# Decoder step kernel: the first weight load on ScalarE's queue, and the second weight chunk loaded in one piece

## The chip, the cores and the metric

The kernel runs on one core of a Trainium2 chip. The time is the device time of one execution in microseconds (us), the median of three runs; lower is better. Engines are named as the profile names them: PE (TensorE, with PEld for its weight loads), DVE (VectorE), ACT (ScalarE), POOL (GpSimd) and SP (SyncE, which here issues DMA transfers). A row such as "SPq" is the time in which a queue issues a DMA, not the transfer itself.

## The reference, cut to what matters

One inference step of a two-layer decoder over 256 prompt tokens and 64 sample tokens (8 groups of 8), width 1024. Layer 0 mixes tokens with a chunked spatial gate, layer 1 with an mLSTM memory; each is followed by a gated MLP with a short causal convolution. The change touches the very start of layer 0 alone: the normalised input times the `v` half of `a_w_in`.

```
def chunk_spatial_gating(x, w_in, ln_g, ln_b, w_s, b_s, w_out):
    bsz, s, _ = x.shape
    h = jax.nn.gelu(x @ w_in)
    u, v = jnp.split(h, 2, axis=-1)
    ...
def trunk(x, ...):
    for i in range(DEPTH):
        h = rmsnorm(x, norm_mix_g[i])
        if i % N_MIXERS == 0:
            y, v = chunk_spatial_gating(h, ...)
        ...
        x = x + y
        h = rmsnorm(x, norm_ffn_g[i])
        y, fb = conv_ffn(h, ...)
        x = x + y
```

## The kernel before

All 320 tokens (T) are worked on together. The activations lie transposed, 128 features to a block, as eight rows of 320 tokens; "x0" to "x7" below are these eight rows, each the transfer of 160 KB that `x_in` issues (line 382), except x0, which is issued in `run` (line 1274) and carries 16 columns of gains as well (336 columns, 168 KB).

Float32 products are made from two parts of each operand, a high one and a low one. So a chunk of weights comes in as `raw`, ACT casts it to the high part `wh` (line 176, or 171 for the first two chunks), and DVE subtracts to get the low part `wl` (lines 177 and 173). For x, `norm_block` makes the high part `xh` on ACT (line 262) and the low part `xl` on DVE (line 263), and POOL copies the 64 sample columns of both into `xs_a` (lines 386 and 387), behind `xl` for the second copy. PE multiplies only these parts (line 80, the helper `mm`).

The list of weights is made in `weights`; `prefetch(n, m)` sees to it that n chunks have been issued for loading and m have been split. "w0" is chunk 0 (block 0 of `a_wv`, the first four of eight feature blocks, 256 KB), "w1" is chunk 1 (block 4, same feature blocks), "w2" is chunk 2 (block 0, the other four feature blocks), "w3" chunk 3, and so on. `raw` has four buffers, so the load of w4 waits until w0 has been split, w5 until w1 has, and so on. `hold` pins instructions of the start to the order in which the program is written.

Only w0 and w1 are handled in halves: each half is two feature blocks, 128 x 256 numbers, 128 KB. Their loads are four transfers on SP, behind x0. In splitting, DVE makes the first high part of w0 itself (line 168) before `x_parts(0)`, and the other three halves' high parts are ACT casts (line 171); the four low parts are DVE's (line 173). `natural`, which is called for groups of 512 output columns (group 0: w0, later w2 and others; group 1: w1), takes the two halves of such a chunk one after the other, with all tokens for the first half before the second half.

Ahead of that work, `run` issues x0, then `prefetch(2, 0)`, then on ACT a one-column activation `warm` (line 1278) with the table load that it needs, and on PE seven products of constants. SP's order at the start is x0, the four halves, x1, w2, x2, w3, x3, w4, and so on, all on one queue.

Of the kernel before, what the change touches and what calls it, by code (L numbers as in the profile page):

```python
# [58 lines left out]
class Net:  # L59
# [84 lines left out]
    def prefetch(self, n, m):  # L144

        nc = self.nc
        while len(self.loaded) < min(n, len(self.wq)):
            w, b, k0, kn = self.wq[len(self.loaded)]
            raw = self.wraw.tile([P, 8, P], F32, tag="raw", name="raw")
            if isinstance(b, tuple):  # L150
                n = kn // len(b)
                for j, m_ in enumerate(b):
                    self.last_load = nc.sync.dma_start(raw[:, j * n:j * n + n, :], w[m_, :, k0:k0 + n, :])
            else:
                for j, z in ((0, 2), (2, 4)) if len(self.loaded) < 2 else ((0, kn),):
                    self.last_load = self.hold(nc.sync.dma_start(raw[:, j:z, :], w[b, :, k0 + j:k0 + z, :]))  # L156
            self.loaded.append(raw)
        while len(self.halved) < min(m, len(self.wq)):
            i = len(self.halved)
            raw, kn = self.loaded[i], self.wq[i][3]  # L160
            self.loaded[i] = None
            wh = self.wsp.tile([P, 8, P], F32R, tag="wh", name="wh")
            wl = self.wsp.tile([P, 8, P], F32R, tag="wl", name="wl")
            if i < 2:

                a, z = slice(0, 2), slice(2, 4)
                if not i:
                    self.hold(nc.vector.tensor_copy(wh[:, a, :], raw[:, a, :]))
                    self.x_parts(0)
                for c in (a, z)[not i:]:  # L170
                    self.last_split = self.hold(nc.scalar.copy(wh[:, c, :], raw[:, c, :]))
                for c in (a, z):
                    self.last_low = self.hold(nc.vector.tensor_tensor(wl[:, c, :], raw[:, c, :], wh[:, c, :].bitcast(F32), op=SUB))
                self.halved.append((wh, wl))
                continue
            self.last_split = self.hold(nc.scalar.copy(wh[:, :kn, :], raw[:, :kn, :]))  # L176
            self.last_low = nc.vector.tensor_tensor(wl[:, :kn, :], raw[:, :kn, :], wh[:, :kn, :].bitcast(F32), op=SUB)  # L177
            self.hold(self.last_low)
            self.halved.append((wh, wl))
# [1227 lines left out]
```

## Time and profile before

| | us |
|---|---|
| median of three runs | 882.41 (882.1 to 882.59) |
| profiled execution, its own time | 883.35 |
| its span, first to last instruction | 881.6 |
| PE busy in the span | 874.3 (99%) |
| DVE, ACT, POOL busy | 670.7, 512.5, 118.8 |
| granted TensorE clock | 0.998 |

A profile row gives the start, the length, the engine, the line, the operation, what it writes and reads, and how many were merged into the row; in brackets at its end stands how long the engine had been idle before it and what released it. Adjacent instructions of one kind are merged, and matmul ends are modelled, so the pace of PE is best read from one start to the next.

### The profile page before, as it was taken

The numbers are of one execution on the slowest core, as the hardware profiler recorded it, in microseconds if no ns is written. First come the engines' busy times: TensorE is split into PE (matmuls) and PEld (weight loads), VectorE is DVE, ScalarE is ACT, GpSimd is POOL, SyncE is SP. The second block draws the span as 40 slices with busy tenths as digits, with TensorE's granted clock in tenths as the row PEclk, the third lists the DMA queues.
The fourth block names the chain that finished last, engine by engine and source line by source line (L and its number), as shares of the span: only waits on it lengthen the run. The fifth ranks groups of instructions, "written<-read, shape, count | busy, mean of one in ns | idle before, by whom it ended". The sixth has DMA issues, their size and how long they took to land.

```text
span 881.6 us, 17001 instructions
## 1 busy us (share of the span) xinstructions
PE 874.3 (99%) x6423; PEld 857.1 (97%) x6423; DVE 670.7 (76%) x1291; ACT 512.5 (58%) x930; POOL 118.8 (13%) x288
## 2 busy tenths in 40 slices
PE   9999999999999999999999999999999999999997
PEld 7889999999999999999999999999999999999997
DVE  5866986678878865558999998878988788786443
ACT  6658554455555544347777775656766555554442
POOL 3300000020000000002433222303001000000000
PEclk9999999999999999999999999999999999999999
DMA  7755645544454455554746876665664544555551
GB/s 248 245 177 166 184 149 169 177 152 161 167 168 156 156 163 168 160 163 149 244 154 225 248 218 223 197 210 169 192 224 145 167 160 153 168 161 164 156 151 60
DMA packets 55238, 155.76 MB, mean 177 GB/s; under 512 B 7492, under 2 KB 13260, under 8 KB 55156
## 3 DMA queue, kind: packets, MB, share of 16 engines
q1 hardware_dynamic: 55156, 154.67, 55.0%
q8 instruction: 51, 0.84, 0.4%
q14 instruction: 31, 0.25, 0.1%
HBM read 142.66 MB, written 11.99 MB: 175 GB/s over the span
## 4 chain that ended last, share of the span: by engine, by line
PE 98%; DMA 1%; SPq 0%; DVE 0%; issue 0%; ACT 0%; POOL 0%; ACTq 0%
PE pm L80 84%; PE pv_a L80 6%; PE num L80 2%; PE pmix L80 1%; PE pcs L80 1%; PE psc L80 1%; DMA raw<-in_a_wv 1%; PE pCp L80 1%; PE phn L83 1%; PE pv L83 1%; PE pc L80 0%; PE pk L83 0%; SPq L156 0%; DVE y_p L686 0%; PE pg L80 0%; PE pb L80 0%
## 5 line engine op out<-in xcount | busy, mean ns | idle before, releaser
L177 DVE TENSOR_TENSOR wl<-raw,wh 128x1024 fp32r<-128x1024 f32 (+4 forms) x254 | 299.3, 1180 | 115.2 <-ACT wh L176 112.5
L176 ACT CAST wh<-raw 128x1024 fp32r<-128x1024 f32 (+4 forms) x254 | 255.5, 1006 | 215.7 <-PE pm L80 145.9
L80 PE MATMUL pm<-xh,wh 128*128 128x320 f32 x1216 | 356.4, 301 | 0.0
L80 PE MATMUL pm<-xl,wh 128*128 128x320 f32 x1216 | 354.5, 299 | 0.0
L80 PE MATMUL pm<-xh,wl 128*128 128x320 f32 x1216 | 308.8, 299 | 0.0
L80 PEld LDWEIGHTS pm<-xh,wh 128*128 128x128 f32 x1216 | 229.9, 189 | 0.1
L80 PEld LDWEIGHTS pm<-xl,wh 128*128 128x128 f32 x1216 | 229.9, 189 | 0.1
L80 PEld LDWEIGHTS pm<-xh,wl 128*128 128x128 f32 x1216 | 212.0, 189 | 0.0
L80 PE MATMUL pm<-yh_f,wh 128*128 128x320 f32 x352 | 105.2, 299 | 0.0
L80 PE MATMUL pm<-yl_f,wh 128*128 128x320 f32 x352 | 105.2, 299 | 0.0
L80 PE MATMUL pm<-yh_f,wl 128*128 128x320 f32 x352 | 105.2, 299 | 0.0
L80 PEld LDWEIGHTS pm<-yh_f,wh 128*128 128x128 f32 x352 | 66.5, 189 | 0.0
L80 PEld LDWEIGHTS pm<-yl_f,wh 128*128 128x128 f32 x352 | 66.5, 189 | 0.0
L80 PEld LDWEIGHTS pm<-yh_f,wl 128*128 128x128 f32 x352 | 66.5, 189 | 0.0
L592 DVE SCALAR_TENSOR_TENSOR fcv<-fpad,vecs,fcv 128x336 f32<-128x336 f32 x88 | 49.6, 565 | 2.1 <-ACT fcv L590 0.7
L594 ACT ACTIVATE fgl<-fcv 128x256 f32<-128x256 f32 x44 | 18.3, 416 | 37.5 <-DVE fcv L592 37.5
L80 PE MATMUL pm<-yh_a,wh 128*128 128x320 f32 x128 | 38.4, 300 | 0.0
L80 PE MATMUL pm<-yl_a,wh 128*128 128x320 f32 x128 | 38.3, 299 | 0.0
L80 PE MATMUL pm<-yh_a,wl 128*128 128x320 f32 x128 | 38.3, 299 | 0.0
L346 DVE TENSOR_TENSOR xT<-pm,xT 128x320 f32<-128x320 f32 x39 | 19.0, 487 | 24.4 <-PE pm L80 24.4
L80 PE MATMUL pm<-yhb,wh 128*128 128x320 f32 x128 | 35.9, 304 | 0.0
L80 PE MATMUL pm<-ylb,wh 128*128 128x320 f32 x128 | 35.5, 300 | 0.0
(272 smaller groups left out, 1262.9 us busy)
## 6 DMA issues: line engine op xcount, KB each, us to landing
raw<-in_f_up SPq DMA_DIRECT2D x88, 512.0 KB, 3.3
raw<-in_b_win SPq DMA_DIRECT2D x48, 512.0 KB, 4.2
raw<-in_f_dn SPq DMA_DIRECT2D x32, 448.0 KB, 3.3
C<-in_C SPq DMA_DIRECT2D x32, 258.0 KB, 5.3
out_Cs<-C SPq DMA_DIRECT2D x32, 258.0 KB, 4.6
raw<-in_a_win SPq DMA_DIRECT2D x16, 512.0 KB, 3.3
raw<-in_a_wo SPq DMA_DIRECT2D x16, 512.0 KB, 3.9
raw<-in_f_dn SPq DMA_DIRECT2D x16, 512.0 KB, 3.6
```

Of the source, the lines that this page charges most:

```text
L80: self.pin(self.nc.tensor.matmul(out, lhsT, rhs, start=start, stop=stop, skip_group_check=skip))
L83: self.pin(self.nc.tensor.transpose(out, in_, ident))
L176: self.last_split = self.hold(nc.scalar.copy(wh[:, :kn, :], raw[:, :kn, :]))
L177: self.last_low = nc.vector.tensor_tensor(wl[:, :kn, :], raw[:, :kn, :], wh[:, :kn, :].bitcast(F32), op=SUB)
L346: self.nc.vector.tensor_tensor(x, ps[:, :T], x, op=ADD)
L592: nc.vector.scalar_tensor_tensor(cv, pd[:, i:i + NC], self.vec(w + i * KF), cv, op0=MULT, op1=ADD)
L594: nc.scalar.activation(gl[:, :TP], cv[:, :TP], AF.Gelu_apprx_tanh)
```

## The change

The loop that issues the loads of single blocks is changed in two places. Halves are used only for chunk 0, so chunk 1 is loaded by one transfer of 128 x 512 numbers (256 KB). The first half of chunk 0 is issued on ACT's DMA queue; everything else stays on SP. How the chunks are split and multiplied is as before: chunk 1's split still runs half by half.

```
@@ -152,8 +152,9 @@
             else:
-                for j, z in ((0, 2), (2, 4)) if len(self.loaded) < 2 else ((0, kn),):
-                    self.last_load = self.hold(nc.sync.dma_start(raw[:, j:z, :], w[b, :, k0 + j:k0 + z, :]))
+                for j, z in ((0, 2), (2, 4)) if not self.loaded else ((0, kn),):
+                    queue = nc.sync if self.loaded or j else nc.scalar
+                    self.last_load = self.hold(queue.dma_start(raw[:, j:z, :], w[b, :, k0 + j:k0 + z, :]))
             self.loaded.append(raw)
```

On SP, at the very start of the program, the rows of before (the loads of x rows are `xT`, those of weights `raw`; 128x256 is half a chunk, 128x512 a chunk):

```order
L1274 DMA xT<-in_xv 128x336
L156 DMA raw<-in_a_wv 128x256 x4
L382 DMA xT<-in_xv 128x320
L156 DMA raw<-in_a_wv 128x512
L382 DMA xT<-in_xv 128x320
L156 DMA raw<-in_a_wv 128x512
L382 DMA xT<-in_xv 128x320
```

The same place on SP in the changed kernel, whose lines from 157 on stand one further down:

```order
L1275 DMA xT<-in_xv 128x336
L157 DMA raw<-in_a_wv 128x256
L157 DMA raw<-in_a_wv 128x512
L383 DMA xT<-in_xv 128x320
L157 DMA raw<-in_a_wv 128x512
L383 DMA xT<-in_xv 128x320
L157 DMA raw<-in_a_wv 128x512
```

Between x0 and x1 there were four issues, and there are two: the second half of w0 and the whole of w1.

On ACT, at the very start, the rows of before:

```order
L1278 ACT_TABLE_LOAD
L1278 ACTIVATE warm<-mhalf 128x1
L262 ACTIVATE xh<-xT 128x320
L171 CAST wh<-raw 128x256 x3
L262 ACTIVATE xh<-xT 128x320
```

And of the changed kernel:

```order
L157 DMA raw<-in_a_wv 128x256
L1279 ACT_TABLE_LOAD
L1279 ACTIVATE warm<-mhalf 128x1
L263 ACTIVATE xh<-xT 128x320
L172 CAST wh<-raw 128x256 x3
L263 ACTIVATE xh<-xT 128x320
```

One row is added at the head, ahead of the table load; the order behind it is the same. PE, DVE and POOL keep their order throughout, and so do ACT and SP behind these places.

## The prediction

> **What bounds the kernel now.** I read the chain of waits first. Its page summary gives the whole span to PE but for a small DMA share:
>
> ```profile
> PE 98%; DMA 1%; SPq 0%; DVE 0%; issue 0%; ACT 0%; POOL 0%; ACTq 0%
> ```
>
> The change touches only the first microseconds, so the next view is the same chain in order of time, from the start to 35 us (start, length, what):
>
> ```profile
> 0.81 0.40 SPq L1274
> ...
> 1.26 0.42 SPq L156
> ...
> 1.72 0.43 SPq L156
> ...
> 2.19 0.43 SPq L156
> ...
> 2.67 0.43 SPq L156
> ...
> 3.14 0.43 SPq L382
> ...
> 3.62 0.43 SPq L156
> ...
> 4.09 0.43 SPq L382
> ...
> 4.57 5.97 DMA raw<-in_a_wv
> ...
> 10.65 0.63 ACT wh L176
> ...
> 11.32 19.26 PE pv_a L80 x88
> ```
>
> Nine issues on SP stand one behind the other, about 0.47 us apart (x0, four halves, x1, w2, x2, w3); the ninth, w3, takes 5.97 us to land; ACT casts it; then PE starts at 11.32 and waits for nothing until after 30 us. So the kernel's end hangs on the landing of w3, at about 10.6 us, one for one: what stands before 11.32 on PE matters only if it becomes later than this chain.
>
> How much slack PE has ahead of 11.32 is read from PE's timeline:
>
> ```profile
> 4.08 0.75 PE L80 MATMUL pv_a<-wh,xh 128*128 128x256 f32 x2
> 4.92 0.43 PE L80 MATMUL pv_a<-wl,xh 128*128 128x256 f32 x2
> 7.98 0.28 PE L80 MATMUL pv_a<-wl,xs_a 128*128 128x256 f32 x1
> 8.74 0.70 PE L80 MATMUL pv_a<-wh,xh 128*128 128x512 f32 x2 [0.49 <-ACT wh L176]
> 11.32 0.70 PE L80 MATMUL pv_a<-wh,xh 128*128 128x512 f32 x2 [0.58 <-ACT wh L176]
> 13.15 0.59 PE L80 MATMUL pv_a<-wh,xh 128*128 128x512 f32 x2
> 14.88 0.59 PE L80 MATMUL pv_a<-wh,xh 128*128 128x512 f32 x2
> ```
>
> A chunk without a wait takes 14.88 - 13.15 = 1.73 us from start to start. The small products step by 0.11 us (7.98 to the end of the block at 8.09). So w2's products start 8.74 - 8.09 = 0.65 late, w3's lose a further 8.74 to 11.32 less 1.73 = 0.85, and 11.32 to 13.15 loses 0.10 more in restarting. The two waits cost 1.60 us; that is all that faster loading of w2 and w3 could return, 0.18% of the time.
>
> **The change part by part.**
>
> *Issues.* SP loses two issues ahead of x1. By the rows above each is 0.47 us from start to start, so x1 goes from 3.14 to about 2.19, w2 from 3.62 to 2.67, w3 from 4.57 to 3.62: 0.95 earlier. Counted on the path at most 0.95, if w3 still needs 5.97 us to land; at least 0, if the DMA engines and not the issues set the landing.
>
> *What ACT gains in work.* One issue ahead of its table load:
>
> ```profile
> 0.80 1.28 ACT L1278 ACT_TABLE_LOAD   x1 [0.80 <-PEq L1387]
> 2.09 0.20 ACT L1278 ACTIVATE warm<-mhalf 128x1 f32<-128x1 f32 x1
> 3.27 0.56 ACT L262 ACTIVATE xh<-xT 128x320 fp32r<-128x320 f32 x1 [0.97 <-DMA xT<-in_xv]
> ```
>
> No DMA is issued by ACT in this trace. By SP's rows the issue takes 0.40 to 0.43; then the table load ends at about 2.5 and `warm` at 2.7. ACT sat idle 0.97 us for x0, so the cost is nothing up to a delay of 0.97; a longer issue would move `xh` one for one. Bounds: 0 and, with three issue times in its place (1.29), 0.32. I take 0, as the nearest row is SP's. Queued behind the issue are the table load, `warm` and `xh`; DVE's `xl`, POOL's copies and PE wait for `xh`.
> [...]
>
> *x0 and the first half of w0 side by side.* What they start is on DVE:
>
> ```profile
> 3.64 0.29 DVE L168 CAST wh<-raw 128x256 fp32r<-128x256 f32 x1 [2.54 <-DMA raw<-in_a_wv]
> 3.86 0.61 DVE L263 SCALAR_TENSOR_TENSOR xl<-xT,xh 128x320 fp32r<-128x320 f32 x1
> 4.40 0.41 DVE L173 TENSOR_TENSOR wl<-raw,wh 128x256 fp32r<-128x256 f32 x1
> ```
>
> Now x0 lands at 3.27 and the first half of w0 at 3.64. The half lands up to 0.46 earlier, but `xl` starts 0.03 behind the end of `xh` (3.27 + 0.56 = 3.83), so the earlier half brings nearly nothing: the pace to PE's 4.92 is xh, xl, wl. Against that, x0 now shares the 16 DMA engines with the half from the first packet. Bounds: x0 at 3.27 as now, or at 3.64, the moment when both have landed today. I take 3.5, about 0.2 later for PE's first block. It is hidden by the wait of 0.65 ahead of w2; if that wait were gone, it would cost 0.2.
>
> *The second chunk in one piece.* Its split and products are unchanged, but the first half's cast now waits for all of it:
>
> ```profile
> 5.56 0.75 ACT L171 CAST wh<-raw 128x256 fp32r<-128x256 f32 x2 [0.56 <-DMA raw<-in_a_wv]
> 6.31 0.39 PE L80 MATMUL pv_a<-wh,xh 128*128 128x256 f32 x2
> ```
>
> Today its first half lands at 5.56 and the second by about 5.9; PE needs the first cast (0.40 long) at 6.31. Whole, between 5.0 (a saved issue and better packets) and 5.9. At 5.9 the cast ends at 6.3: just in time with PE 0.2 later. Cost 0, at worst some 0.3, again inside the 0.65.
>
> *The landing of w3* is the term that reaches the end. The stretches of one microsecond (columns: stretch, sum, busy of PE, PEld, DVE, ACT, POOL, clock, DMA share, GB/s) show how full the DMA engines were:
>
> ```profile
> 2.00:3.00 1.00, 1.00 (x4) 0.37 (x3) 0.00 (x0) 0.28 (x2) 0.30 (x2) 1.00 0.80 261
> 3.00:4.00 1.00, 0.98 (x3) 0.07 (x1) 0.36 (x2) 0.56 (x1) 0.11 (x1) 1.00 0.69 175
> 4.00:5.00 1.00, 0.92 (x5) 0.95 (x6) 0.81 (x2) 0.40 (x1) 0.50 (x2) 1.00 1.03 266
> 6.00:7.00 1.00, 1.00 (x12) 1.00 (x11) 0.77 (x2) 0.31 (x1) 0.00 (x0) 1.00 0.94 252
> 9.00:10.00 1.00, 1.00 (x6) 0.86 (x6) 0.42 (x1) 0.08 (x1) 0.00 (x0) 1.00 1.05 378
> ```
>
> From 4 us on they are full, so most of the 0.95 is not to be had: w3 queues behind data, not behind issues. Two things are. Between 2 and 4 us shares of 0.20 and 0.31 lay idle while SP was issuing small pieces; with the work there sooner, 0 to 0.51 us comes back, and I take 0.3. And w1 goes in 2 KB runs per partition where it went in 1 KB runs: eight packets fewer for each of 16 engines (128 of them in all). The packet counts (packets, MB, share of 16 engines), of 4 to 5 us, of 5 to 7 and of 9 to 10, price a packet:
>
> ```profile
> q1 hardware_dynamic: 281, 0.27, 103.4%
> ...
> q1 hardware_dynamic: 351, 0.49, 92.7%
> ...
> q1 hardware_dynamic: 253, 0.38, 105.0%
> ```
>
> 16 x 1.034 / 281 = 59 ns at 0.96 KB; 32 x 0.927 / 351 = 85 ns at 1.4 KB; 16 x 1.05 / 253 = 66 ns at 1.5 KB. By the first and the third a packet costs 13 ns more per KB, so 2 KB takes 73 ns, and eight of these in place of sixteen of 59 save 0.37 us. By the first and the second 2 KB takes about 120 ns, and nothing is saved. I take 0.2, the middle.
>
> *The sum.* w3 lands 0.3 + 0.2 = 0.5 earlier (bounds 0 and 0.95), at about 10.1; PE starts it at 10.8 rather than 11.32. PE itself would be ready at 8.09 + 0.2 + 1.73 = 10.0, so the landing still rules. Behind it, ACT works w3, x3 and w4 off in a row (10.65 to 12.38 today), so w4 moves along with w3, and PE, which took it at 13.15, keeps 0.77 us of slack. Nothing else changes; PE is continuous from there. The profiled execution: 883.35 - 0.5 = 882.85 (span 881.1). It lies 0.94 above the median of the runs, so for the median 882.41 - 0.5 = 881.9.
>
> **The rivals.**
>
> *Nothing arrives sooner (the transfer is bound by data).* The shares of 0.91 to 1.05 from 4 to 11 us speak for it, the idle shares before 4 against it. w3 lands at 10.6 as now: 882.4.
> [...]
>
> *Both waits go.* x2, the row ahead of w3, landed 5.8 us after its issue:
>
> ```profile
> 9.92 0.56 ACT L262 ACTIVATE xh<-xT 128x320 fp32r<-128x320 f32 x1 [1.23 <-DMA xT<-in_xv]
> ```
>
> If that lateness is a pile-up on a few engines that the earlier start dissolves, w3 lands more than 0.95 earlier and up to 1.60 returns; the 0.2 by which x0 is later is then on the path, so 1.4 is left: 881.0. Against it: w4's load still waits for w0's split, and ACT's row of casts would soon be what PE waits for.
>
> *The earlier crowd drains slower.* With two queues served at once from the first packet and w0, w1, x1, w2, x2, w3 all issued by 4.1 rather than 5.0 us, each engine changes between queues and has more in flight. The place is the DMA engines from 2 to 10 us, the price the rate: x0 to w3 are 1512 KB (168, four times 128, twice 160, twice 256), 1.55 MB, landed by 10.6. Moved from 2.0 to 10.6, that is 180 GB/s for what w3 needs; 10% less costs 0.86 us. As w3's landing has no slack, it decides from the first nanosecond that exceeds what is gained: 882.41 + 0.9 = 883.3. For it: 175 GB/s in the 3 to 4 us row, while small pieces of several transfers were in flight. Against it: the best rates, 378, stand where the backlog is longest.
>
> *The change does not do what it says:* were ACT's issue to come late, the half would land where it did, and w3 still profits from the shorter list on SP; that lies inside the forecast's range.
>
> **How the numbers follow.** The forecast, 0.25 to 0.95 earlier, has 0.55: 881.9, by itself 881.4 to 882.2. Nothing sooner has 0.25 (882.2 to 882.7), both waits gone 0.07 (880.8 to 881.4), the slower crowd 0.13 (882.7 to 883.7). Holding eight in ten and a scatter of 0.25 us as in the runs of before, the range is 881.0 to 883.0. A change under 0.2%, 1.8 us, is what a measurement of this kernel cannot tell from none, and none of the cases' middles passes it: even the full 1.60 stays within. What could is a mishap or a windfall at the cases' ends: faster 0.06, within 0.86, slower 0.08.
>
> **What would show it right or wrong.** Right: on SP, w3 is issued at about 3.6 and ACT's cast of it starts near 10.1; PE's third chunk starts near 10.8 and the waits ahead of it shrink but remain; the DMA share from 2 to 4 us rises from 0.80 and 0.69 to about 0.95; ACT's `xh` starts a little later than 3.27 and DVE's first cast earlier than 3.64, ahead of `xl` and without use. Wrong: w3's landing where it was, or later, with w3 issued at 3.6 (the rivals bound by data or by the crowd); ACT's issue longer than 0.97 us; a wait on PE behind 13 us that was not there; or a difference in the later stages, where no order has changed.

## The result, and the profile after

The changed kernel is slower: 884.02 us median over 21 runs (882.42 to 884.49) against 882.27 (881.63 to 882.87) for the kernel before. The ratio of the runs is 1.0013, with a 95% interval of 1.0008 to 1.0019. That is within the 0.2% named in the prediction, but on the other side of zero than the 881.9 forecast, and above the range of 881.0 to 883.0. The times do not lie around one value: 6 of the 21 are at 882.4 to 882.8 (the lower group below), two near 883.2, and 13 at 883.8 to 884.5 (the upper group).

The chain of waits of the changed kernel, in order of time, starts differently from that of the kernel before:

```profile
0.81 3.13 DMA xT<-in_xv
...
3.96 0.57 ACT xh L263
...
4.58 27.03 PE pv_a L80 x128
```

The chain no longer passes through w3. PE starts on the landing of x0 and from 4.58 us on waits for nothing: the two waits ahead of w2 and w3 are gone. And yet it gets further behind. PE's timeline of the same execution (start, length, engine, line, operation, what it writes and reads, count):

```profile
0.84 3.15 PE L80 MATMUL pw<-const-bfloat16-1.0 128*128 128x512 bf16 x7 [0.84 <-PEq L1388]
4.58 0.79 PE L80 MATMUL pv_a<-wh,xh 128*128 128x256 f32 x2 [0.59 <-ACT xh L263]
...
6.23 0.42 PE L80 MATMUL pv_a<-wh,xs_a 128*128 128x256 f32 x1
6.44 0.42 PE L80 MATMUL pv_a<-wl,xs_a 128*128 128x256 f32 x1
6.66 0.63 PE L80 MATMUL pv_a<-wh,xh 128*128 128x256 f32 x2
...
8.36 0.63 PE L80 MATMUL pv_a<-wh,xh 128*128 128x256 f32 x2
...
9.61 0.27 PE L80 MATMUL pv_a<-wh,xs_a 128*128 128x256 f32 x1
9.72 0.28 PE L80 MATMUL pv_a<-wl,xs_a 128*128 128x256 f32 x1
...
10.72 0.60 PE L80 MATMUL pv_a<-wh,xh 128*128 128x512 f32 x2
...
14.18 0.59 PE L80 MATMUL pv_a<-wh,xh 128*128 128x512 f32 x2
```

The same engine in the kernel before:

```profile
0.84 3.14 PE L80 MATMUL pw<-const-bfloat16-1.0 128*128 128x512 bf16 x7 [0.84 <-PEq L1387]
...
5.30 0.28 PE L80 MATMUL pv_a<-wl,xs_a 128*128 128x256 f32 x1
5.41 0.39 PE L80 MATMUL pv_a<-wh,xh 128*128 128x256 f32 x2
...
6.31 0.39 PE L80 MATMUL pv_a<-wh,xh 128*128 128x256 f32 x2
```

In the changed kernel, from 6.23 to 6.44, a product of 256 columns takes 0.21 us from start to start; from 9.61 to 9.72 it takes 0.11, as it did from 5.2 us on before (5.30 to 5.41). Eight products, half a chunk, take 8.36 - 6.66 = 1.70 us rather than 0.90 (6.31 - 5.41). Nothing is waited for in between. PE runs its first real products at half pace, until about 9.4 us. The stretch from 6 to 7 us says it in one row (busy of PE, PEld, DVE, ACT, POOL, granted clock, DMA share, GB/s):

```profile
6.00:7.00 1.00, 1.00 (x7) 1.00 (x6) 0.00 (x0) 0.36 (x2) 0.00 (x0) 1.00 1.01 367
```

PE is busy all of the time with 7 products where the prediction's row of the kernel before has 12, and the column of the granted clock reads 1.00 in both. The transfers are not the brake here: 367 GB/s against 252.

Ahead of it stand ACT and DVE, which show when x0 and the first half of w0 landed:

```profile
0.81 0.40 ACTq L157 DMA_DIRECT2D raw<-in_a_wv  x1
1.24 1.28 ACT L1279 ACT_TABLE_LOAD   x1 [1.24 <-PEq L1388]
...
3.96 0.56 ACT L263 ACTIVATE xh<-xT 128x320 fp32r<-128x320 f32 x1 [1.22 <-DMA xT<-in_xv]
...
6.64 0.71 ACT L172 CAST wh<-raw 128x256 fp32r<-128x256 f32 x2 [1.82 <-DMA raw<-in_a_wv]
...
8.96 0.62 ACT L177 CAST wh<-raw 128x512 fp32r<-128x512 f32 x1
```

```profile
4.13 0.29 DVE L169 CAST wh<-raw 128x256 fp32r<-128x256 f32 x1 [3.04 <-DMA raw<-in_a_wv]
```

x0 lands at 3.96 rather than 3.27, and the half, although issued 0.45 us earlier, at 4.13 rather than 3.64. Both are later than when they stood one behind the other. The products of constants end at 3.99 as before, so PE is idle for 0.59 us where it was idle for about 0.1. The cast of w3 on the other hand begins at 8.96 rather than 10.65.

So there were two things to explain: the half pace, and the late x0. Theory A was that the idle gap ahead of the first real product causes the half pace. Its rivals were that the late x0 is the loss by itself, or that the crowd of transfers slows the start.

### The profile page after: what moved, and what is told of

It reads as the page before. It is cut to its first block, busy times and chain, and to the rows that moved or that the text cites. A ratio compares the mean times of both kernels' runs of the same rounds, so it can differ in the third digit from the quotient of the medians.

```text
span 882.5 us, 16999 instructions
## 1 busy us (share of the span) xinstructions
PE 875.9 (99%) x6423; PEld 859.1 (97%) x6423; DVE 670.8 (76%) x1291; ACT 511.8 (58%) x930; POOL 117.2 (13%) x288
## 4 chain that ended last, share of the span: by engine, by line
PE 99%; DMA 0%; DVE 0%; ACT 0%; POOL 0%; issue 0%
PE pm L80 84%; PE pv_a L80 7%; PE num L80 2%; PE pmix L80 1%; PE pcs L80 1%; PE psc L80 1%; PE pCp L80 1%; PE phn L83 1%; PE pv L83 1%; PE pc L80 0%; DMA xT<-in_xv 0%; PE pk L83 0%; DVE y_p L687 0%; PE pg L80 0%; PE pb L80 0%; PE pr L80 0%
```

## The experiments

Each experiment has a short name, such as e1. All times are medians of 11 runs with the kernel before run beside them, unless a single execution is named. The kernel before had medians of 882.38 to 882.40 in the three sets that were timed.

### The gap closed, and the gap opened

Two kernels change nothing but the number of products of constants. In the changed kernel, nine in place of seven (e1):

```
-            for i in range(7):
+            for i in range(9):
                 self.mm(pw, one[:, :P], one, True, True)
```

> The changed kernel with nine products of constants ahead of the first real one instead of seven, so that PE is not idle between 3.9 and 4.6 us. Theory A (the idle gap makes PE run its first real products at half pace): no gap, steps of 0.11 us per 256-column product from 7.7 us at the latest, and a time of about 881.9 us (881.2 to 882.9), below the changed kernel by 1 to 2.5 us. Theory B (x0's late landing itself is the loss, PE's pace has another cause): steps of 0.21 us until 9 us as in the changed kernel, and 884.0 us or a little more.

Measured 882.78 us (882.39 to 883.09), ratio 1.0004 (0.9995 to 1.0012). The upper group of times is gone. PE's timeline:

```profile
2.50 2.34 PE L80 MATMUL pw<-const-bfloat16-1.0 128*128 128x512 bf16 x5
4.75 0.61 PE L80 MATMUL pv_a<-wh,xh 128*128 128x256 f32 x2
...
6.28 0.39 PE L80 MATMUL pv_a<-wh,xh 128*128 128x256 f32 x2
...
7.17 0.39 PE L80 MATMUL pv_a<-wh,xh 128*128 128x256 f32 x2
```

x0 landed as late as in the changed kernel (ACT's first `xh` at 4.14), but half a chunk takes 7.17 - 6.28 = 0.89 us: full pace. Later loads with a later start cost little; the half pace was the loss. The time came out 0.9 above the middle expected.

In the kernel before, five in place of seven (e2):

> The kernel before with five products of constants instead of seven; nothing else differs. They end near 3.1 us, so PE is idle for about 0.9 us before its first real product at 4.05. Theory A: that product and those behind it run at half pace (0.21 us) for some 4 us, the start of w2's products moves from 8.74 to about 11, and after the 1.60 us of waiting that this uses up the time is 883.3 to 884.5 us. Theory B: the loads are untouched, so 882.3 us.

Measured 883.37 us (882.90 to 884.61), ratio 1.0013 (1.0004 to 1.0022), with every load as before:

```profile
4.08 0.77 PE L80 MATMUL pv_a<-wh,xh 128*128 128x256 f32 x2 [0.95 <-DVE wh L168]
...
5.92 0.64 PE L80 MATMUL pv_a<-wh,xh 128*128 128x256 f32 x2
...
7.62 0.63 PE L80 MATMUL pv_a<-wh,xh 128*128 128x256 f32 x2
...
10.55 0.60 PE L80 MATMUL pv_a<-wh,xh 128*128 128x512 f32 x2
```

PE starts at 4.08 as ever, behind a gap of 0.95 us, and half a chunk takes 1.70. This is a loss like that of the change, without any part of the change: the ratio is the same 1.0013, though by the medians it is 1.0 us rather than 1.75. Theory A stands; the rivals, which leave this kernel at 882.3, do not explain the half pace.

With six products of constants in the kernel before (e6):

> The kernel before with six products of constants: PE idles about 0.5 us before its first real product at 4.05. Theory A with a limit on the idle time between the 0.28 us that did no harm and the 0.59 that did: part of the runs at half pace for some 4 us, so two groups of times, near 882.4 and near 884, as the changed kernel shows. Theory B, that any gap does harm in proportion: one group near 883.

Measured 883.91 us, ratio 1.0011 (1.0002 to 1.0020), and times spread over 882.2 to 884.4 rather than in two clean groups. The profiled execution had a gap of 0.57 us and half pace (start of w2's products at 10.65). Three of the 11 runs are at 882.2 to 882.8, so a gap of this size does not cost the time in every execution; no profile shows what is different in those.

The control, nine products of constants in the kernel before:

> The kernel before with nine products of constants instead of seven, the control for e1_after_nine. They end near 4.8 us, so the first real product starts at about 4.75 rather than 4.05. Theory A: no gap, no half pace behind 5 us, the later start is mostly taken from the waits ahead of w2 and w3: 882.3 to 882.9 us. Theory B, that more products of constants speed PE up by themselves: below 882.0.

Measured 882.70 us (882.29 to 883.07), ratio 1.0000 (0.9991 to 1.0009). So two more products of constants gain nothing by themselves, and with the gap closed in both, the kernel before and the changed one are at 882.70 and 882.78: the change itself, without its gap, is worth nothing that these runs can tell.

### The two edits apart

The second chunk in one piece, all on SP (e3):

```
-                    queue = nc.sync if self.loaded or j else nc.scalar
+                    queue = nc.sync
```

> The second chunk in one piece, everything on SP: the change without ScalarE's queue. Theory A: x0 lands at 3.3 us as before, PE starts at 4.05 without a gap, w3 is issued one step earlier, and the time is 881.7 us (881.2 to 882.3). Theory B, that the one piece and the crowd of transfers in flight are what makes the start slow: 883 us or more, with x0 later than 3.5.

Measured 882.09 us (881.88 to 882.37), ratio 0.9997 (0.9988 to 1.0005): not told apart from the kernel before, 0.3 us below it by the medians. x0 landed at 3.52, the gap was 0.28 us, the pace was full, and there was no wait ahead of w2 or w3. There was one ahead of w1, whose products could have started at 6.56:

```profile
4.28 0.46 PE L80 MATMUL pv_a<-wh,xh 128*128 128x256 f32 x2 [0.28 <-DVE wh L169]
...
6.83 0.49 PE L80 MATMUL pv_a<-wh,xh 128*128 128x256 f32 x2
...
8.73 0.60 PE L80 MATMUL pv_a<-wh,xh 128*128 128x512 f32 x2
...
12.19 0.59 PE L80 MATMUL pv_a<-wh,xh 128*128 128x512 f32 x2
```

ScalarE's queue alone, with the second chunk in halves:

```
-                for j, z in ((0, 2), (2, 4)) if not self.loaded else ((0, kn),):
+                for j, z in ((0, 2), (2, 4)) if len(self.loaded) < 2 else ((0, kn),):
```

> ScalarE's queue for the first half, the second chunk in two halves on SP as before: the change without the one piece. Theory A: x0 lands near 3.9 us since two queues start at once, PE idles about 0.6 us and runs at half pace for some 4 us; w3 is issued at 4.1; 883.4 to 884.5 us. Theory B: x0 lands at 3.3 and the time is that of before or below, 881.9 to 882.4.

Measured 884.17 us (882.36 to 884.83), ratio 1.0017 (1.0008 to 1.0026): the whole loss. Its profiled execution:

```profile
4.74 0.78 PE L80 MATMUL pv_a<-wh,xh 128*128 128x256 f32 x2 [0.75 <-ACT xh L263]
...
8.51 0.64 PE L80 MATMUL pv_a<-wh,xh 128*128 128x256 f32 x2
```

The edit that costs is the queue. One piece with eight products of constants, to see whether the best of both is below the kernel before:

> The second chunk in one piece on SP, without ScalarE's queue, and eight products of constants. Theory A: no gap ahead of the first real product, all runs at full pace from 5 us, w3 lands earlier than in the kernel before: 881.6 to 882.1 us, the lowest of all. Theory B, that the saved issue is lost again to data that arrives no sooner: 882.4 us.

Measured 882.38 us (881.91 to 882.88), ratio 0.9998 (0.9989 to 1.0007): no gain, so no version here beats the kernel before. In its profiled execution PE was never idle from 0.84 us on, and still ran at half pace until about 6.4 us (half a chunk from 4.10 to 5.93, the next to 7.07); in e1, also without a gap, the steps were 0.11 from 6.05 on.

### What the waits of the kernel before were worth

> The kernel before, unchanged, for another profile. Its profiled execution of 883.35 us lay above all its other runs. If the 1.60 us of waits ahead of w2 and w3 belong to every run, this profile shows them again; if they belong to that execution, a run of 882.4 us shows some 0.9 us less of them, with w3 at 10.4 us rather than 11.3.

> As e9_before_again, a second time: a profile of some 882.4 us with waits ahead of w2 and w3 of about 0.7 us together rather than 1.6.

The two executions took 882.36 and 882.39 us, spans of 880.7. PE's timeline of the second:

```profile
4.14 0.46 PE L80 MATMUL pv_a<-wh,xh 128*128 128x256 f32 x2 [0.15 <-DVE wh L168]
...
7.30 0.39 PE L80 MATMUL pv_a<-wh,xh 128*128 128x256 f32 x2
...
8.62 0.70 PE L80 MATMUL pv_a<-wh,xh 128*128 128x512 f32 x2 [0.27 <-ACT wh L176]
...
10.46 0.60 PE L80 MATMUL pv_a<-wh,xh 128*128 128x512 f32 x2
...
12.18 0.59 PE L80 MATMUL pv_a<-wh,xh 128*128 128x512 f32 x2
```

The first two chunks end at 7.30 + 0.89 = 8.19, so w2's products are 0.43 late and lose 0.11 more in restarting: 0.54 us, not 1.60. In the first it is 0.30 (8.42 to 10.35 and 12.18 without a wait ahead of w2). In the second execution ACT casts w3 from 9.17, in the first from 9.68, not from 10.65. The profile from which the prediction was made was of an execution with a later w3 than either.

These profiles also give the account of the loss. The start of w4's products is the mark behind which nothing differs: 12.18 here with a span of 880.7, 13.15 with 881.6, 14.18 with 882.5, a constant distance of 868.3 to 868.5. From this profile to that of the changed kernel PE's start moves by 4.58 - 4.14 = 0.44, the first two chunks take 10.72 - 4.58 = 6.14 rather than 8.19 - 4.14 = 4.05, that is 2.09 more, and the waits give back 0.54: 1.99, against 14.18 - 12.18 = 2.00.

### Why x0 lands late

A small load on ScalarE's queue in the kernel before: the mask `mk`, 128 rows of 32 bytes, 4 KB, in place of the first half, which stays on SP. The mask's load later in the program is left out.

```
+            self.hold(nc.scalar.dma_start(self.mk, I["blk"]))
             self.prefetch(2, 0)
```

> The kernel before, with one small load (the 4 KB mask mk, 128 rows of 32 bytes) issued on ScalarE's queue ahead of the table load instead of later on SP. It tells why x0 lands late. Theory A1 (two queues that start at once hold each other up, whatever they carry): x0 lands at 3.6 us or later, PE idles 0.4 us or more, part of the runs at half pace, 883 us or more. Theory A2 (x0 shares bandwidth with the 128 KB of the first half): x0 lands at 3.2 to 3.35 as before and the time is 882.4 us.

Measured 882.25 us (881.85 to 882.92), ratio 0.9997 (0.9988 to 1.0005). x0 landed at 3.51 in its one profile, between the two expectations; the profiles with all loads on SP range from 3.11 to 3.52. A second queue in use is not by itself what delays x0 by 0.7 us or more; a smaller delay is not excluded. The gap was 0.31 us and the pace full from 5.7 us.

ScalarE's issue behind the table load and `warm` (e13):

```
-            self.prefetch(2, 0)
             nc.vector.memset(self.mhalf, -0.5)
             warm = cp.tile([P, 1], F32, name="warm")
-            nc.scalar.activation(warm, self.mhalf, AF.Gelu_apprx_tanh)
+            self.hold(nc.scalar.activation(warm, self.mhalf, AF.Gelu_apprx_tanh))
+            self.prefetch(2, 0)
```

> The changed kernel with ScalarE's issue of the first half moved behind the table load and the one-column activation, to about 2.3 us, so that x0 starts alone; on SP x1 moves ahead of w1. Theory A2 (x0 is late because it shares its first microsecond with the half): x0 lands at 3.1 to 3.5 us again, the half at 4.3 or later, so PE still idles and runs at half pace, 884 us. Theory A1' (any use of the second queue makes x0 late): x0 lands at 3.9 us or later.

It did not come out as either theory had it, because the issue did not go where it was meant to go. ACT's timeline:

```profile
0.81 1.28 ACT L1278 ACT_TABLE_LOAD   x1 [0.81 <-PEq L1388]
0.97 0.38 ACTq L157 DMA_DIRECT2D raw<-in_a_wv  x1
2.10 0.20 ACT L1278 ACTIVATE warm<-mhalf 128x1 f32<-128x1 f32 x1
3.60 0.56 ACT L263 ACTIVATE xh<-xT 128x320 fp32r<-128x320 f32 x1 [1.30 <-DMA xT<-in_xv]
```

Though the program now places it behind the activation on ACT, the transfer was issued at 0.97 us, while the table load ran. With x0 only 0.16 us ahead, x0 lands at 3.60 and the half at 3.96 (DVE's cast). The one execution took 882.32 us, with a gap of 0.41 and full pace. Timed:

> The kernel of e13_issue_late again, timed. In its one look ACT issued the half at 0.97 us, during the table load, x0 landed at 3.60, PE idled 0.41 us and went on at full pace. Theory A (an idle gap near 0.4 to 0.6 us decides the pace): most runs near 882.3, some above 883.5 where x0 is later, a median of 882.3 to 883.0. Theory B, that the later issue frees the start altogether: all runs below 882.3.

Measured 883.89 us (882.31 to 884.66), ratio 1.0010 (1.0001 to 1.0019). Six of 11 runs are at 883.89 or above, so the median lies above what A had expected, and e13 had shown one of the quicker runs. The profiled execution had x0 at 3.69:

```profile
4.48 0.77 PE L80 MATMUL pv_a<-wh,xh 128*128 128x256 f32 x2 [0.50 <-DVE wh L169]
...
6.39 0.63 PE L80 MATMUL pv_a<-wh,xh 128*128 128x256 f32 x2
...
8.10 0.64 PE L80 MATMUL pv_a<-wh,xh 128*128 128x256 f32 x2
...
9.61 0.39 PE L80 MATMUL pv_a<-wh,xh 128*128 128x256 f32 x2
```

A gap of 0.50 us rather than 0.41, and half pace until about 9 us. With an eighth product of constants (e18):

> The same with eight products of constants, which end near 4.4 us and so close the gap of 0.41 us. Theory A: no run above 883.2, a median of 882.0 to 882.6. Theory B, that the gap plays no part in this kernel: the same spread as e17_issue_late_timed.

Measured 882.82 us (882.41 to 883.18), ratio 1.0002 (0.9993 to 1.0011), no run above 883.2. PE's timeline:

```profile
4.74 0.59 PE L80 MATMUL pv_a<-wh,xh 128*128 128x256 f32 x2 [0.32 <-DVE wh L169]
...
7.67 0.49 PE L80 MATMUL pv_a<-wh,xh 128*128 128x256 f32 x2 [0.52 <-ACT wh L172]
```

x0 landed at 3.95, as late as in the changed kernel, and the eighth product did not close the gap but kept it at 0.32 us; the pace was full from 5.9 us. The gap decides here as well. The median is 0.2 above what A had given; in this profile PE also waits 0.52 us for w1, which stands behind x1 on SP in this kernel.

### The changed kernel again

> The changed kernel, unchanged, for another profile. Its times fall into two groups, near 882.5 and near 884.2. A run of the lower group shows, by theory A, real products at full pace from 6 us at the latest, after a shorter idle gap or after the same; one of the upper group half pace until 9 us or later.

> As e11_after_again, a second time: the lower group with full pace from 6 us, or the upper with half pace until 9 us.

> The changed kernel, unchanged, for a profile of its lower group of times (882.4 to 882.8 us), which 6 of its first 21 runs belong to. Theory A: in such a run the first real products reach full pace within about 2 us of PE's start, though the idle gap is the same. Theory B: in such a run x0 lands at 3.3 us and there is no gap.

> As e14_after_again: if it falls into the lower group, full pace early (theory A) or x0 early (theory B).

> As e14_after_again: if it falls into the lower group, full pace early (theory A) or x0 early (theory B).

The five executions took 883.96, 884.45, 883.79, 884.33 and 884.78 us: all in the upper group or near it, so the lower group was never profiled, and what makes 6 of 21 runs quick stays open. In the five x0 landed at 4.54, 4.43, 4.08, 4.21 and 4.15, the gaps were 1.17, 1.06, 0.70, 0.84 and 0.78 us, and all ran at half pace at first, until about 8 to 10 us. The longest gap did not bring the longest half pace: behind 1.17 us it ended at about 8.2, behind 0.78 at about 10.1. The kernel before, too, has 3 of its 87 runs beside these experiments at 883.86 to 884.45; none of these was profiled either.

## Why the prediction was wrong

**The bound.** The prediction put the end of the kernel on the landing of w3, "one for one", and the slack ahead of it at 1.60 us. That reading of its profile was right for that execution. But it subtracted the gain from the median, while it had noted that the execution lay 0.94 above it. In executions of 882.4 the waits are worth 0.30 to 0.54: most of what was to be gained was not in the typical run. This term was mis-sized, 1.60 for about 0.4, and the 0.5 that was taken off for w3 was about all that a typical execution had to give.

**Issues and the landing of w3.** SP's part went as worked out: w3 is issued at 3.66 rather than 4.57. The landing of w3 moved from 10.65 to 8.96 at the latest against the profile used, and from 9.17 to 8.96 against a typical one; the forecast of 0.5 is between the two. The cost of 0 for ACT's issue was right: it took 0.40 us, the table load ended at 2.5, and ACT sat idle 1.22 us for x0.

**x0 beside the half.** This is the first step that failed. The prediction bounded x0's landing between 3.27 and 3.64, "the moment when both have landed today", and took 3.5. It was 3.96 to 4.54 in the six profiles of the changed kernel. The upper bound assumed that two transfers together take no longer side by side than in a row. Here they did: the half landed later too, at 4.13 to 4.72. The stretches of the changed kernel at that place:

```profile
2.00:3.00 1.00, 1.00 (x4) 0.37 (x3) 0.00 (x0) 0.72 (x2) 0.30 (x2) 1.00 0.82 179
3.00:4.00 1.00, 0.99 (x3) 0.08 (x1) 0.00 (x0) 0.04 (x1) 0.00 (x0) 1.00 1.01 346
```

From 2 to 3 us the engines are as busy as before (0.82 and 0.80) and move 179 rather than 261 GB/s; from 3 to 4 they move 346 rather than 175. More had been moved by 4 us than before, but the pieces that PE needed first were not whole. The packets of 2 to 3 us (packets, MB, share of 16 engines), of the kernel before and then of the changed one, show on which queue the time went:

```profile
q1 hardware_dynamic: 236, 0.26, 80.4%
...
q1 hardware_dynamic: 90, 0.12, 64.3%
q10 hardware_dynamic: 58, 0.06, 17.6%
```

q1 is SP's queue, and q10 is ScalarE's, which carries the half alone. A packet on SP's queue, x0's among them, took 16 x 0.643 / 90 = 114 ns, where it had taken 16 x 0.804 / 236 = 55 ns with 1.1 KB rather than 1.3 KB in it; one on ScalarE's queue took 49 ns. In the seven other profiles with both issues at 0.8 us the engines moved 152 to 183 GB/s from 2 to 3 us, at shares of 0.70 to 0.87, and in the seven others with all loads on SP 240 to 275, at 0.79 to 0.88. So x0 lost its time in transfer, between 2 and 3 us, while the half moved beside it. Why it is SP's packets that are slowed was not settled.

**PE's pace.** The step that cost the sign: the prediction held that x0's delay "is hidden by the wait of 0.65 ahead of w2". It counted PE at 0.11 us per product, whenever it starts. The experiments show that an idle gap ahead of the first real products costs this pace. In all 20 profiles the two go together: with no gap or one of up to 0.41 us PE was at full pace within 2.4 us of its first real product, and with gaps of 0.50 us and more it stayed at half pace until 8 to 10 us. Opening the gap alone cost 1.0 us (e2); closing or shortening it took the upper group away (e1, e18). The timed runs say that it is not certain in every execution (three of e6, six of the changed kernel were quick). The cover of 0.65 was used up by the half pace, which is 2.09 us.
The two paces are a factor of two apart (0.21 and 0.11 us for 256 columns), and behind gaps of 0.50 us and more the turn from one to the other came 3 to 6 us after PE's first real product. Full pace was not lost in the gap: the 3.1 us of products of constants ahead of it step by 0.43 us for 512 columns themselves, against 0.22 later. How a gap of 0.50 us puts full pace off was not shown: the granted clock of the profile reads 1.00 all along.

**The second chunk in one piece** cost nothing and brought nothing that the times can tell (e3). But it was to land by 5.9 us at the latest, and ACT casts it from 6.64 in the changed kernel. There the half pace hides it, since PE comes to w1 at 8.36; at full pace, in e3, PE lost 0.27 us to it (6.83 rather than 6.56), near the worst case of 0.3 that the prediction named.

**The rivals.** "Nothing arrives sooner" fell, since w3 landed sooner. The slower crowd fell at the place that it named, w3's landing, but a slower crowd there was, at x0: 179 rather than 261 GB/s from 2 to 3 us. The engines did serve two queues in the same microsecond, SP's for 80.0% and ScalarE's for 21.2% of the time of the 16 from 3 to 4 us; what a change between queues costs was not shown. "Both waits go" came true, and the kernel was slower all the same, since PE had become the bound at half pace. None of them held PE's half pace.

## What to carry to other kernels

Here the products that keep TensorE going ahead of the first real work had to reach nearly up to it: in one kernel, e13 and e17, an idle time of 0.41 us behind them left full pace within 1.0 us, and one of 0.50 us half pace until about 9 us. When a load of the start is moved, check the idle time between the last of them and the first real product, and add one or two (0.43 us each here) if it nears half a microsecond. Two transfers that are both needed first were better issued in a row on one queue than at the same moment on two; that is shown here for 168 and 128 KB, which had both landed by 3.84 us at the latest in a row and by 4.13 at the earliest together. And a gain that is read from waits in one profile is to be checked against a second profile whose time is the median.

## What the runs showed of the hardware that was not expected

- TensorE at half pace (0.21 us rather than 0.11 for 256 columns) for 3 to 6 us behind an idle gap of 0.50 to 1.17 us, and for at most 2.4 us behind one of up to 0.41 us, with the profile's granted clock at 1.00 throughout. The pace is seen in the steps from start to start, not in the clock column.
- Two transfers of 168 and 128 KB issued at the same time on two queues landed at 3.96 to 4.54 and 4.13 to 4.72 us; in a row on one queue, 0.45 us apart, at 3.11 to 3.52 and 3.62 to 3.84.
- While two queues were loaded at once, in the changed kernel, a packet on SP's queue took 114 ns between 2 and 3 us, against 55 ns with SP's queue alone in the kernel before; one on ScalarE's took 49 ns.
- A transfer that the program places behind an activation on ScalarE was issued 0.16 us after the table load began, while it ran, and ahead of that activation.
